# The opening loads of a one-core decoder layer, spread anew over two DMA queues

## The chip, the core and the metric

The kernel runs on one core of a Trainium2 chip. The metric is device time in microseconds for one execution. A core has five engines with instruction streams of their own: TensorE (PE in the profile; its weight loads are PEld), VectorE (DVE), ScalarE (ACT), GpSimd (POOL) and SyncE (SP). Transfers between the chip's main memory and the core's on-chip memory are issued as instructions in an engine's stream (SPq and ACTq in the profile are such issues on SyncE's and ScalarE's streams) and are then moved by 16 DMA engines, which serve both queues.

## The reference

One decoder layer over 256 tokens of width 2048, in float32: a norm, one wide projection, two parallel branches (a short convolution and a gated recurrence), a gated merge and an output projection, then a per-layer embedding and a final norm.

```python
    h = rmsnorm(x, norm_mix_g[i])
    u = h @ w_in[i]
...
    m = jax.nn.sigmoid(ga) * (ya @ w_a_out[i]) + jax.nn.sigmoid(gb) * (yb @ w_b_out[i])
    x = x + m @ w_o[i]
    gate = jax.nn.sigmoid(rmsnorm(x, ple_norm_g[i]) @ w_ple_gate[i])
    x = x + gate * (p[i] @ w_ple_proj[i])
return rmsnorm(x, final_norm_g)
```

The change concerns only how the inputs of `p[i] @ w_ple_proj[i]` reach the core. That product depends on nothing else, so the kernel does it first. `p` is 256 tokens by 256 features and `w_ple_proj` is 256 by 2048.

## The kernel before

**How a product is made.** Float32 accuracy comes from splitting each operand into a high part in the reduced format fp32r and the remainder. `cut` (lines 199 and 200) does this for weights: ScalarE copies the loaded tile `raw` to `whi`, then VectorE subtracts to get `wlo`. Each product is then three matmuls of 128 x 128 by 128 x 512: high by high, high weights by low operand, and low weights by high operand (lines 1157 to 1159). The contraction dimension goes in k tiles of 128.

**The list of weight pieces.** The weights are worked off as a fixed list of items, in an order written down in the code. Items 0 to 3 are the four groups of 512 columns of `w_pp` (`w_ple_proj`). Each is 128 partitions by 1024 numbers: the first 512 of a row belong to k tile 0 and the last 512 to k tile 1. The text calls the two halves of item 0 W0a and W0b, those of item 1 W1a and W1b, and so on to W3b; one half is 256 KB. `p` is laid out transposed with features on partitions. Its two k tiles, 128 KB each, are called p0 and p1; they go to the tile `praw`, and their split parts to `pop`.

**The first twelve matmuls** (line 1312) are those of item 0. For k tile 0 there are two matmuls (for two blocks of 128 tokens) with the high part of W0a and the high part of `pop`, two with the high part of W0a and the low part of `pop`, and two with the low part of W0a. The same six follow for k tile 1 with W0b and p1. Before these, TensorE runs eight matmuls on a zeroed tile `warm` (line 1046), which compute nothing that is used.

**Order on the engines.** Each engine works its own stream in order. ScalarE's stream starts with its DMA issues, then a load of its function table with a first activation (line 303), then the split of W0a, the high part of p1 (line 325), the split of W0b, W1a, W1b, W2a, W2b and, in one instruction, item 3. VectorE does the high part of p0 (line 323), its low part (line 326), and then the low parts in the same order as ScalarE. The parameters `prm_t` (norm gains, convolution weights and the like) are first read when the layer's input is split (line 328).

**A limit on transfers in flight.** The transfers that SyncE and ScalarE issue take turns over eight completion semaphores, DMAHW0 to DMAHW7. A transfer that uses a semaphore again waits, in its issuing engine's stream, until the transfer eight places before it has landed. The count runs over both queues together, roughly in the order of the program text.

Of the kernel before, what the change touches and what calls it, by code (L numbers as in the profile page):

```python
# [15 lines left out]
P = 128  # L16
T = 256
# [6 lines left out]
CW = 512  # L24
# [24 lines left out]
def hybrid_kernel(ctx, tc, xT, x, pT, prm, gfin, masks, w_in, w_a, w_b, w_o, w_pg, w_pp, out):  # L49
    nc = tc.nc  # L50
# [27 lines left out]
    def nm(s):  # L78
        uid[0] += 1
        return f"{s}_{uid[0]}"  # L80
# [26 lines left out]
    items = []  # L107
# [21 lines left out]
    def raw_of(pos):  # L129
        it = items[pos]  # L130
        if it["raw"] not in loaded:
            if it["kind"] == "S" and it["op"] == "hT":
                t = tuple(
                    pools["st"].tile([P, n, CW], F32, tag=tag, bufs=bufs, name=nm(tag))
                    for tag, n, bufs in (("sA", 2, 2), ("sB", 1, 3))
                )
            else:
                n = it["c"] if it["j"] == 0 else 4 + 4 * (it["j"] - 1) + it["c"] // 2
                spare = it["op"] == "x1T" and n in (5, 10, 14)
                pool, bufs = (pools["late"], 1) if spare else (wp, 3)  # L140
                t = pool.tile([P, 2, 2 * CW], F32, tag="raw", bufs=bufs, name=nm("raw"))
            loaded[it["raw"]] = t
        return loaded[it["raw"]]
# [117 lines left out]
    prm_t = const.tile([P, PRM_N], F32, name="prm_t")  # L261
    praw = pools["tmp1"].tile([P, 1024], F32, tag="X", bufs=4, name="praw")[:, : 2 * T]
# [10 lines left out]
    def load_half(pos, i, eng):  # L273
        w, g, c = items[pos]["w"]
        s = slice(i * CW, (i + 1) * CW)
        eng.dma_start(out=raw_of(pos)[:, pos % 2, s], in_=w[g, :, c, s])

    load_half(0, 0, nc.scalar)
    for k in range(2):
        nc.sync.dma_start(out=praw[:, k * T : (k + 1) * T], in_=pT[:, k, :])  # L280
    load_half(0, 1, nc.scalar)
    for i in range(2):
        load_half(1, i, nc.sync)
    nc.sync.dma_start(out=prm_t, in_=prm)
    for c in (2, 3):
        for i in range(2):
            load_half(c, i, nc.sync)
# [938 lines left out]
    for pos, it in enumerate(items[:last_group]):  # L1226
        mark, state["pos"] = len(nc.cur_bb.bb.instructions), pos
        kind, j, c, last = (it[n] for n in ("kind", "j", "c", "last"))
        _, _, w, g, opname = groups[it["gi"]]
# [71 lines left out]
        else:  # L1301
# [4 lines left out]
            for i in range(2):  # L1306
                k = 2 * c + i
# [50 lines left out]
    for t, halves in ((0, (0, 1)), (1, (0,)), (1, (1,))):  # L1358
        bk, n = bank("g"), CW // 2
        for c in range(nlast):  # L1360
# [4 lines left out]
            for i in range(2):  # L1365
                k = 2 * c + i
# [87 lines left out]
```

## Time and profile before

| | |
|---|---|
| median of 3 runs | 813.72 us (812.8 to 813.87) |
| profiled execution, its time | 812.97 us |
| profiled execution, its span | 811.2 us |
| TensorE busy | 801.2 us, 99% |
| VectorE, ScalarE, GpSimd busy | 605.9, 462.9, 55.0 us |
| first matmul whose result is used | 5.05 us after the span's start |

The span runs from the first to the last instruction in the trace; the time of an execution also has what lies around it, here 1.77 us. Rows of the timeline give the start, the duration, the engine, the line, the operation and the tiles, with a count where equal instructions were merged, and in square brackets how long the engine was idle before it and what ended that. A matmul's duration includes the pipeline, so the pace of TensorE is read from the distance of starts.

### The profile page before, as it was taken

The numbers are of one execution on the slowest core, as the hardware profiler recorded it, in microseconds if no ns is written. First come the engines' busy times: TensorE is split into PE (matmuls) and PEld (weight loads), VectorE is DVE, ScalarE is ACT, GpSimd is POOL, SyncE is SP. The second block draws the span as 40 slices with busy tenths as digits, with TensorE's granted clock in tenths as the row PEclk, the third lists the DMA queues.
The fourth block names the chain that finished last, engine by engine and source line by source line (L and its number), as shares of the span: only waits on it lengthen the run. The fifth ranks groups of instructions, "written<-read, shape, count | busy, mean of one in ns | idle before, by whom it ended". The sixth has DMA issues, their size and how long they took to land.

```text
span 811.2 us, 10709 instructions
## 1 busy us (share of the span) xinstructions
PE 801.2 (99%) x4053; PEld 663.7 (82%) x4053; DVE 605.9 (75%) x785; ACT 462.9 (57%) x624; POOL 55.0 (7%) x59
## 2 busy tenths in 40 slices
PE   9999999999999999999999999999999999999995
PEld 6888888888888888888888888888888888888885
DVE  6846588767776498767679987987988666789953
ACT  7676476465555466466456556556554446665733
POOL 1000000001000000000021210110000000000160
PEclk9999999999999999999999999999999999999999
DMA  9988555648767555647799996995844778896702
GB/s 337 392 312 292 194 204 170 230 141 267 256 236 257 182 187 200 207 160 261 271 313 309 305 327 206 304 329 194 249 158 174 284 271 277 309 349 245 297 27 103
DMA packets 54099, 198.52 MB, mean 245 GB/s; under 512 B 6944, under 2 KB 16928, under 8 KB 40352
## 3 DMA queue, kind: packets, MB, share of 16 engines
q1 hardware_dynamic: 44640, 174.78, 60.5%
q0 software_dynamic: 6384, 16.25, 8.4%
q10 hardware_dynamic: 3024, 6.82, 2.4%
q8 instruction: 31, 0.51, 0.2%
q14 instruction: 20, 0.16, 0.1%
HBM read 184.19 MB, written 13.63 MB: 244 GB/s over the span
## 4 chain that ended last, share of the span: by engine, by line
PE 98%; issue 1%; DMA 0%; ACT 0%; DVE 0%; POOLq 0%; POOL 0%
PE g L1157 27%; PE g L1158 27%; PE g L1159 27%; PE s L1157 5%; PE s L1158 4%; PE s L1159 4%; PE s L539 1%; DMA raw<-in_w_pp 0%; PE g L1312 0%; PE s L640 0%; PE s L659 0%; PE s L658 0%; PE s L657 0%; PE s L631 0%; ACT xs L1006 0%
## 5 line engine op out<-in xcount | busy, mean ns | idle before, releaser
L200 DVE TENSOR_TENSOR wlo<-raw,whi 128x1024 fp32r<-128x1024 f32 (+1 forms) x255 | 304.0, 1209 | 141.1 <-ACT whi L199 139.1
L199 ACT ACTIVATE whi<-raw 128x1024 fp32r<-128x1024 f32 (+1 forms) x255 | 262.1, 1045 | 186.8 <-PE g L1159 158.1
L1157 PE MATMUL g<-whi,xh 128*128 128x512 f32 (+1 forms) x656 | 253.1, 386 | 0.0
L1159 PE MATMUL g<-whi,xl 128*128 128x512 f32 (+1 forms) x656 | 252.7, 385 | 0.0
L1158 PE MATMUL g<-wlo,xh 128*128 128x512 f32 (+1 forms) x656 | 252.7, 385 | 0.0
L1159 PEld LDWEIGHTS g<-whi,xl 128*128 128x128 f32 x656 | 123.2, 188 | 24.9
L1157 PEld LDWEIGHTS g<-whi,xh 128*128 128x128 f32 x656 | 123.2, 188 | 24.6
L1158 PEld LDWEIGHTS g<-wlo,xh 128*128 128x128 f32 x656 | 123.2, 188 | 24.2
L1158 PE MATMUL s<-wlo,xh 128*128 128x512 f32 x120 | 46.7, 389 | 0.0
L1157 PE MATMUL s<-whi,xh 128*128 128x512 f32 x120 | 46.5, 389 | 0.0
L1159 PE MATMUL s<-whi,xl 128*128 128x512 f32 x120 | 46.5, 389 | 0.0
L1158 PE MATMUL g<-wlo,mh 128*128 128x512 f32 x112 | 43.6, 389 | 0.0
L1159 PE MATMUL g<-whi,ml 128*128 128x512 f32 x112 | 43.5, 390 | 0.0
L1157 PE MATMUL g<-whi,mh 128*128 128x512 f32 x112 | 43.1, 389 | 0.0
L199 ACT ACTIVATE thi<-sA 128x1024 fp32r<-128x1024 f32 x15 | 15.9, 1062 | 32.8 <-DVE sA L756 20.3
L1159 PEld LDWEIGHTS s<-whi,xl 128*128 128x128 f32 x120 | 22.5, 188 | 4.7
L1157 PEld LDWEIGHTS s<-whi,xh 128*128 128x128 f32 x120 | 22.5, 188 | 4.7
L1158 PEld LDWEIGHTS s<-wlo,xh 128*128 128x128 f32 x120 | 22.5, 188 | 4.7
L1158 PE MATMUL g<-wlo,ybTh 128*128 128x512 f32 x64 | 24.9, 389 | 0.0
L1159 PE MATMUL g<-whi,ybTl 128*128 128x512 f32 x64 | 24.9, 389 | 0.0
L1157 PE MATMUL g<-whi,yaTh 128*128 128x512 f32 x64 | 24.9, 389 | 0.0
L1158 PE MATMUL g<-wlo,yaTh 128*128 128x512 f32 x64 | 24.9, 389 | 0.0
(272 smaller groups left out, 1075.8 us busy)
## 6 DMA issues: line engine op xcount, KB each, us to landing
raw<-in_w_in SPq DMA_DIRECT2D x66, 1024.0 KB, 4.8
raw<-in_w_o SPq DMA_DIRECT2D x16, 1024.0 KB, 6.3
sT<-in_w_in POOLq DMA_DIRECT2D x30, 512.0 KB, 9.5
raw<-in_w_in SPq DMA_DIRECT2D x28, 512.0 KB, 5.7
raw<-in_w_a SPq DMA_DIRECT2D x8, 1024.0 KB, 7.8
raw<-in_w_b SPq DMA_DIRECT2D x8, 1024.0 KB, 8.7
raw<-in_w_pg SPq DMA_DIRECT2D x16, 512.0 KB, 6.6
raw<-in_w_pg SPq DMA_DIRECT2D x8, 1024.0 KB, 6.7
```

The lines of the kernel that those rows point to most:

```text
L199: a = nc.scalar.activation(out=hi, in_=src, func=AF.Copy)
L200: v = nc.vector.tensor_tensor(out=lo, in0=src, in1=hi.bitcast(F32), op=ALU.subtract)
L539: nc.tensor.matmul(out, X[:, 0, h, s], X[:, 1, h, t], start=True, stop=True, tile_position=(0, i * n))
L1157: nc.tensor.matmul(psum, oh, hi, start=first, stop=False)
L1158: nc.tensor.matmul(psum, oh, lo, start=False, stop=False)
L1159: nc.tensor.matmul(psum, ol, hi, start=False, stop=last)
```

## The change

Four things are changed in the opening loads. W0a, until now one transfer on ScalarE's queue, becomes two: partitions 0 to 95 on ScalarE's queue and partitions 96 to 127 on SyncE's. p1 moves from SyncE's queue to ScalarE's, ahead of W0b. The parameters move from SyncE's queue to the end of ScalarE's opening issues. All the other transfers keep their queue and order.

```diff
-    load_half(0, 0, nc.scalar)
-    for k in range(2):
-        nc.sync.dma_start(out=praw[:, k * T : (k + 1) * T], in_=pT[:, k, :])
+    def load_p(k, eng):
+        eng.dma_start(out=praw[:, k * T : (k + 1) * T], in_=pT[:, k, :])
+
+    def load_rows(i, eng):
+        r, (w, g, c) = (slice(0, 96), slice(96, P))[i], items[0]["w"]
+        eng.dma_start(out=raw_of(0)[r, 0, :CW], in_=w[g, r, c, :CW])
+
+    load_rows(0, nc.scalar)
+    load_p(0, nc.sync)
+    load_p(1, nc.scalar)
+    load_rows(1, nc.sync)
     load_half(0, 1, nc.scalar)
+    nc.scalar.dma_start(out=prm_t, in_=prm)
     for i in range(2):
         load_half(1, i, nc.sync)
-    nc.sync.dma_start(out=prm_t, in_=prm)
```

ScalarE's stream at the start of the program reads as follows before the change; `raw_85` holds items 0 and 1, `raw_93` items 2 and 3, and the wait in brackets names the semaphore.

```order
L276 DMA raw_85<-in_w_pp 128x512 x2
L303 ACT_TABLE_LOAD
L303 ACTIVATE table_113<-mhalf 128x8 [waits Pool_49]
L199 ACTIVATE whi_136<-raw_85 128x512 [waits DMAHW0_49]
L325 ACTIVATE pop<-praw 128x256 [waits DMAHW2_49]
L199 ACTIVATE whi_136<-raw_85 128x512 [waits DMAHW3_49]
L199 ACTIVATE whi_144<-raw_85 128x512 [waits DMAHW4_49]
```

The same place of ScalarE's stream after the change (line numbers behind the edit are 8 higher):

```order
L283 DMA raw_85<-in_w_pp 96x512
L279 DMA praw<-in_pT 128x256
L276 DMA raw_85<-in_w_pp 128x512
L290 DMA prm_t<-in_prm 128x72
L311 ACT_TABLE_LOAD
L311 ACTIVATE table_114<-mhalf 128x8 [waits Pool_49]
L199 ACTIVATE whi_137<-raw_85 128x512 [waits DMAHW2_49,DMAHW0_49]
L333 ACTIVATE pop<-praw 128x256 [waits DMAHW3_49]
L199 ACTIVATE whi_137<-raw_85 128x512 [waits DMAHW5_49]
L199 ACTIVATE whi_145<-raw_85 128x512 [waits DMAHW4_49]
```

Four issues instead of two stand ahead of the table load, and the split of W0a waits for two transfers instead of one.

SyncE's stream at the start of the program, before the change (`raw_98` is the first tile of `w_in`):

```order
L280 DMA praw<-in_pT 128x256 x2
L276 DMA raw_85<-in_w_pp 128x512 x2
L284 DMA prm_t<-in_prm 128x72
L276 DMA raw_93<-in_w_pp 128x512
L276 DMA raw_93<-in_w_pp 128x512 [waits DMAHW0_49]
L276 DMA raw_93<-in_w_pp 128x512 [waits DMAHW1_49]
L276 DMA raw_93<-in_w_pp 128x512 [waits DMAHW2_49]
L276 DMA raw_98<-in_w_in 128x512 [waits DMAHW3_49]
```

The same place of SyncE's stream after the change:

```order
L279 DMA praw<-in_pT 128x256
L283 DMA raw_85<-in_w_pp 32x512
L276 DMA raw_85<-in_w_pp 128x512 x2
L276 DMA raw_94<-in_w_pp 128x512 [waits DMAHW0_49]
L276 DMA raw_94<-in_w_pp 128x512 [waits DMAHW1_49]
L276 DMA raw_94<-in_w_pp 128x512 [waits DMAHW2_49]
L276 DMA raw_94<-in_w_pp 128x512 [waits DMAHW3_49]
L276 DMA raw_99<-in_w_in 128x512 [waits DMAHW4_49]
```

W1a and W1b now have 32 rows of W0a ahead of them instead of p1. There is one transfer more among the opening ones, so W2a is now the ninth of the count and waits for the first transfer to land, which it did not before; every later one waits for a transfer that is one place further back. The streams of TensorE, VectorE and GpSimd, and all of SyncE's and ScalarE's behind this place, are the same but for the numbering.

## The prediction

> **What bounds the kernel now.** I read the page first, its span, its busy times and the chain that ended last, since a change in the opening loads can only matter through what the chain shows at its start.
>
> ```profile
> span 811.2 us, 10709 instructions
> PE 801.2 (99%) x4053; PEld 663.7 (82%) x4053; DVE 605.9 (75%) x785; ACT 462.9 (57%) x624; POOL 55.0 (7%) x59
> PE 98%; issue 1%; DMA 0%; ACT 0%; DVE 0%; POOLq 0%; POOL 0%
> ```
>
> TensorE is the bound. Next come the chain in order of time, at its start, and the waits of TensorE over the whole span.
>
> ```profile
> 0.74 3.61 DMA raw<-in_w_pp
> 4.37 0.64 ACT whi L199
> 5.05 3.04 PE g L1312 x12
> 8.09 0.23 PE g L1157
> ```
>
> ```profile
> PE s L1046 <- DVE warm L1042: 1.2, 1, 1.2
> PE g L1312 <- ACT whi L199: 0.3, 1, 0.3
> ```
>
> So W0a's landing and its split set the first useful matmul at 5.05 us. From there on TensorE waits for nothing that the profile shows. Whatever moves the start, or opens a gap before the lead of the other engines has grown, moves the end by as much; anything else is hidden. The diff changes no other work, so the question is one of tenths of a microsecond. The timeline of that stretch, ScalarE and TensorE, shows how much there is to win or lose.
>
> ```profile
> 0.74 0.89 ACTq L276 DMA_DIRECT2D raw<-in_w_pp  x2
> 1.66 1.28 ACT L303 ACT_TABLE_LOAD   x1 [1.66 <-PEq L1443]
> 2.96 0.21 ACT L303 ACTIVATE table<-mhalf 128x8 f32<-128x8 f32 x1
> 4.37 0.63 ACT L199 ACTIVATE whi<-raw 128x512 fp32r<-128x512 f32 x1 [1.21 <-DMA raw<-in_w_pp]
> 4.96 0.42 ACT L325 ACTIVATE pop<-praw 128x256 fp32r<-128x256 f32 x1
> 5.36 0.63 ACT L199 ACTIVATE whi<-raw 128x512 fp32r<-128x512 f32 x1
> 6.42 2.08 ACT L199 ACTIVATE whi<-raw 128x512 fp32r<-128x512 f32 x3 [0.42 <-DMA raw<-in_w_pp]
> ```
>
> ```profile
> 1.19 3.59 PE L1046 MATMUL s<-warm 128*128 128x512 bf16 x8 [1.19 <-DVE warm L1042]
> 5.05 1.20 PE L1312 MATMUL g<-whi,pop 128*128 128x512 f32 x4 [0.27 <-ACT whi L199]
> 6.55 1.09 PE L1312 MATMUL g<-whi,pop 128*128 128x512 f32 x4
> 7.93 0.39 PE L1157 MATMUL g<-whi,pop 128*128 128x512 f32 x1
> ```
>
> The zero matmuls hold TensorE until 1.19 + 3.59 = 4.78, so an earlier W0a can win 5.05 - 4.78 = 0.27 us and no more. On the other side, W0b's split ends at 5.36 + 0.63 = 5.99, and TensorE needs it at 6.55: about 0.5 us of cover, counting the 0.05 us from a split's end to the matmul (4.37 + 0.63 = 5.00 to 5.05).
>
> **The change part by part.** The landing times come from the DMA issues, asked for in narrow windows (the last number is us from issue to landing; in the first window both were issued at 0.74, the ACTq row of the second is W0b, the praw row p1, the SPq row W1a).
>
> ```profile
> raw<-in_w_pp ACTq DMA_DIRECT2D x1, 256.0 KB, 3.6
> praw<-in_pT SPq DMA_DIRECT2D x1, 128.0 KB, 3.4
> ...
> raw<-in_w_pp ACTq DMA_DIRECT2D x1, 256.0 KB, 4.2
> raw<-in_w_pp SPq DMA_DIRECT2D x1, 256.0 KB, 4.7
> praw<-in_pT SPq DMA_DIRECT2D x1, 128.0 KB, 3.8
> ```
>
> W0a lands at 4.34, p0 at 4.14. W0b, issued second on ScalarE's queue, some 0.45 us after the first, lands at about 5.36, just when ScalarE is free for it. How the two queues share the engines is read from the DMA queues' packets in two stretches, 1.9 to 3.3 and 3.3 to 4.9 us (q10 is ScalarE's queue, q1 SyncE's; packets, MB, share).
>
> ```profile
> q10 hardware_dynamic: 122, 0.23, 45.3%
> q1 hardware_dynamic: 149, 0.14, 31.8%
> ...
> q10 hardware_dynamic: 165, 0.29, 54.7%
> q1 hardware_dynamic: 156, 0.16, 30.6%
> ```
>
> While W0a (rows of 2 KB) runs against p0 (rows of 1 KB), the queues move about as many packets each, but nearly twice the bytes on ScalarE's. So they take turns by packets rather than bytes.
>
> *W0a in two parts.* Its last 32 rows now stand behind p0's 128 rows: packet 160 of SyncE's queue. At 149 packets in 1.4 us, 106 per us, that is 1.5 us after the start; W0a's 128 packets now end at 122 / 1.4 = 87 per us, 1.47 us after the start. With each transfer's 16 further packets (two transfers make 122 + 165 = 287, 144 each) the counts are 192 and 144, so 1.8 and 1.65 us. The last rows thus land 0 to 0.15 later; I take +0.1, so the split at 4.47 and the first matmul at 5.15. The ends: -0.3, if bytes and not packets were shared (192 KB on each queue then, where p1 now shares W0a's time), and +0.45, if the 64 KB of the 32 rows go at SyncE's 0.14 / 1.4 = 0.1 MB per us (0.65 us behind p0, which lands 0.2 us before W0a).
>
> *Two more issues on ScalarE.* At 0.89 / 2 = 0.45 us each they push the table load from 1.66 to 2.55 and the first activation's end to 4.06. The idle 1.21 us before the split covers it; without that cover it costs up to 0.9 us. It also caps the gain: no split before 4.06.
>
> *p1 on ScalarE's queue.* Its 128 KB go behind 96 rows instead of behind p0 and beside W0a: landing 4.6 to 5.0 against 4.97. ScalarE needs it when W0a's split ends, 5.1, so nothing either way.
>
> *W0b behind p1.* Here lies the cost. ScalarE's queue must now move 96 + 128 + 128 = 352 rows until W0b is there, not 256. At 287 packets in 3.0 us, 96 per us, 96 more are +1.0 us. By bytes it is 576 KB against 512 at 0.52 / 3.0 = 0.17 MB per us: +0.4 us. The packet rows are nearer to the first, and W1a with its 2 KB rows is then the opponent on SyncE's queue, where p1 with 1 KB rows was; that could make it +1.4. I take +0.85: landing at 6.2, split until 6.84, matmul at 6.89 instead of 6.55, **+0.34 us**. The 0.1 us from W0a lies inside this, since the k tile 1 matmuls wait for the later of the two. The ends: 0 (+0.4 is under the cover of 0.5) and +0.9.
>
> *Behind it.* W1a has 64 KB instead of 128 ahead of it on SyncE's queue and lands no later; its split runs right after W0b's, 6.84 to 7.47, and TensorE wants it at 7.93 + 0.34 = 8.27. *The parameters* leave SyncE's queue: their issue is worth 0.43 us there, and the first reader stands far behind.
>
> ```profile
> 2.60 0.43 SPq L284 DMA_DIRECT2D prm_t<-in_prm  x1
> 3.07 0.43 SPq L276 DMA_DIRECT2D raw<-in_w_pp  x1
> ...
> raw<-in_w_pp SPq DMA_DIRECT2D x1, 256.0 KB, 4.8
> ...
> 4.37 0.80 SPq L276 DMA_DIRECT2D raw<-in_w_pp  x2
> ...
> 10.57 1.06 ACT L199 ACTIVATE whi<-raw 128x1024 fp32r<-128x1024 f32 x1 [0.79 <-DMA raw<-in_w_pp]
> 12.54 0.91 ACT L328 ACTIVATE xh<-t,prm_t 128x256 fp32r<-128x256 f32 x2 [0.42 <-DMA t<-in_xT]
> ...
> 10.65 0.39 PE L1157 MATMUL s<-whi,pop 128*128 128x512 f32 x1
> 13.37 0.39 PE L1157 MATMUL s<-whi,pop 128*128 128x512 f32 x1
> ```
>
> *One transfer more in the count of eight.* W2a, issued at 3.07 now, must wait for the first 96 rows, until 4.0 to 4.4. Even with the latency of 4.8 us that its issue now has it then lands by 9.2 and is split by 9.9; TensorE uses it at 10.65. What follows is issued one place, some 0.45 us, later: item 3's split would start at 11.0 instead of 10.57 and end at 12.1, against a use at 13.37. So this is hidden; the queue holds megabytes of work anyhow.
>
> **The sum.** W0a 0.1, which lies inside W0b's 0.34, and 0 for all the rest: +0.3 us. Against the profiled execution, 811.2 us of span and 1.77 around it, that is 813.3; its 812.97 lay 0.75 below the median of the runs, 813.72, and from that median I forecast 814.0. A measurement of this kernel can tell about 0.2% from no change, 1.6 us; this is 0.04%.
>
> The Trainium skill, "DMA: Bandwidth & Descriptors", section "Rules for kernel authors", says that two transfers to disjoint partitions are not worth it, because both are spread over the same 16 engines. The packet rows above fit that, as both queues were served in the same stretches; by this rule alone the split of W0a moves its landing by nothing, which is the second rival.
>
> **The rivals.** *The start is won (faster).* If the bytes are shared evenly, W0a lands up to 0.3 us earlier and W0b's delay stays under its cover. The 0.27 us idle before the first matmul speaks for it, the packet counts against it: -0.1 to -0.3, 813.5. It decides if W0b lands before 5.85 and W0a before 4.3. *Nothing moves.* W0a lands as now, W0b is late by less than 0.5: 813.7. For it speaks the byte rate of ScalarE's queue, which alone gives +0.4. *TensorE's clock comes up later.* The zero matmuls start 3.59 / 8 = 0.45 us apart, the later ones 0.23. If gaps of half a microsecond at 4.8 and 6.6 put the faster pace off by as long as the zero matmuls lasted, 3.6 us at half pace cost 1.8 us more: with the slip 816. Against it: the first four useful matmuls take 1.20 us together, the fast pace, in spite of the idle 0.27 ahead of them. The Trainium skill, "TensorE: Matmul & The Clock Gate", Part 1, names a window of about 3.4 us without work as what takes the clock back; by it gaps under 1 us would not, and no run here shows one yet.
>
> **How the numbers follow.** The slip of 0.1 to 1.0 us: 0.50. Nothing moves: 0.18. The start is won: 0.25. The clock or a much later landing: 0.07. Leaving out the last and some of the scatter of the runs (812.8 to 813.87), the range goes from the won start with low runs, 812.9, to the slip at its upper end with a late landing, 815.2. Beyond 0.2% lie only the clock case (0.05 of it) and, on the other side, 0.02 for something that the trace does not show, since the start has only 0.27 us to give.
>
> **What would show it.** Right: W0b's split starts between 5.8 and 6.8 on ScalarE, with an idle time before it ended by the transfer, and TensorE has a second wait of 0.1 to 0.9 us in the middle of the twelve matmuls. Table load at about 2.55, its activation over by 4.1. W2a issued behind the first landing, at 4.0 to 4.4, and no wait of TensorE after 9 us. Wrong: a first matmul before 4.95 with no gap behind it; starts 0.45 us apart in the first twelve; or a wait at items 2 or 3, if the count of eight costs more than I gave it.

## The result, and the profile after

The changed kernel takes 814.56 us (median of 21 runs, 813.62 to 817.84), the kernel before 813.02 us (median of 21, 812.74 to 815.47). The ratio is 1.0018, with an interval from 1.0013 to 1.0024: about 1.5 us more, five times the 0.3 us of the forecast. The time lies inside its range of 812.9 to 815.2.

The chain that ended last, at its start in the changed kernel, no longer runs through W0a (line numbers are 8 higher than before):

```profile
0.74 0.43 ACTq L283
...
1.20 0.45 ACTq L279
...
1.67 5.01 DMA raw<-in_w_pp
...
6.70 0.64 ACT whi L199
```

It runs through ScalarE's first issues to its third transfer, W0b, and the split of that. The waits of TensorE over the span show the same thing as a second, longer wait for a split on the same line, now that of W0b:

```profile
PE s L1054 <- DVE warm L1050: 1.2, 1, 1.2
PE g L1320 <- ACT whi L199: 1.0, 2, 0.7
```

ScalarE's timeline in the changed kernel, to be laid beside the one of before:

```profile
2.64 1.28 ACT L311 ACT_TABLE_LOAD   x1 [2.64 <-issue]
3.93 0.21 ACT L311 ACTIVATE table<-mhalf 128x8 f32<-128x8 f32 x1
4.38 0.63 ACT L199 ACTIVATE whi<-raw 128x512 fp32r<-128x512 f32 x1 [0.24 <-DMA raw<-in_w_pp]
4.92 0.40 ACT L333 ACTIVATE pop<-praw 128x256 fp32r<-128x256 f32 x1
6.70 2.79 ACT L199 ACTIVATE whi<-raw 128x512 fp32r<-128x512 f32 x5 [1.39 <-DMA raw<-in_w_pp]
```

W0a's split starts at 4.38 us, where it was 4.37. W0b's split starts at 6.70 instead of 5.36, behind an idle time of 1.39 us that the transfer ended. TensorE's timeline shows what that does, the last row being the first matmul on `w_in` (behind the four items of `w_pp`):

```profile
5.06 1.20 PE L1320 MATMUL g<-whi,pop 128*128 128x512 f32 x4 [0.35 <-ACT whi L199]
7.38 1.20 PE L1320 MATMUL g<-whi,pop 128*128 128x512 f32 x4 [0.67 <-ACT whi L199]
17.06 0.61 PE L1165 MATMUL g<-whi,xh 128*128 128x512 f32 x2
```

The same matmul on `w_in` in the kernel before:

```profile
16.09 0.62 PE L1157 MATMUL g<-whi,xh 128*128 128x512 f32 x2
```

The matmuls of k tile 1 start 0.83 us late (7.38 for 6.55), the first on `w_in` 0.97. This profiled execution took 813.81 us, 0.84 more than that of before: all of its loss is there by 17 us. It was among the quickest of the changed kernel's runs, so further traces of the same kernel were needed for the rest of the 1.5 us.

### The profile page after: what moved, and what is told of

It is laid out like the page before. It is cut to its first block, busy times and chain, and to the rows that moved or that the text cites. A ratio compares the mean times of both kernels' runs of the same rounds, so it can differ in the third digit from the quotient of the medians.

```text
span 812.0 us, 10711 instructions
## 1 busy us (share of the span) xinstructions
PE 801.3 (99%) x4053; PEld 663.7 (82%) x4053; DVE 605.4 (75%) x785; ACT 462.8 (57%) x624; POOL 55.0 (7%) x59
## 4 chain that ended last, share of the span: by engine, by line
PE 97%; issue 1%; DMA 1%; ACT 0%; DVE 0%; ACTq 0%; POOLq 0%; POOL 0%
PE g L1165 27%; PE g L1167 27%; PE g L1166 27%; PE s L1165 5%; PE s L1167 4%; PE s L1166 4%; DMA raw<-in_w_pp 1%; PE s L547 1%; PE s L648 0%; PE s L667 0%; PE s L666 0%; PE s L665 0%; PE g L1320 0%; PE s L639 0%; ACT xs L1014 0%
```

## The experiments

All ratios are to runs of the kernel before on the same chip, each with its 95% interval.

**More traces of both kernels.** The changed kernel without an edit, twice, and the kernel before once more.

> The changed kernel itself, once more, for a second trace of it. Its first trace has a span 0.8 us longer than before, but the median of its runs is 1.5 us longer. Theory 1 (W0b is late behind p1 on ScalarE's queue, and by how much differs from execution to execution): W0b's split starts after 6.2 us, TensorE has a wait in the middle of the twelve matmuls of 0.3 to 3 us, and the execution's time is that of before plus this wait plus 0.1 to 0.3. Rival (something else in the run differs, such as TensorE's pace): the wait accounts for less than half of what the execution is longer.

> The changed kernel once more, beside the two variants on the same chip, with a third trace. Theory: W0b lands between 6.5 and 7.4 us, and the profiled execution is longer than a fast execution of before (813.0) by W0b's landing less 5.9 us, plus 0.1 for the restart of TensorE and plus whatever waits of TensorE the trace shows elsewhere. Rival: the execution is longer by more than 0.5 us beyond that.

> The kernel before itself, for a second trace of it and as a measure of how far one trace differs from another. Theory: W0a and W0b land within 0.4 us of the first trace (4.34 and 5.36 us), TensorE has no wait in the middle of the twelve matmuls, no difference in time within 0.1%. Rival (the first trace was a lucky one): W0b lands after 6 us here too, with a wait of TensorE.

The changed kernel came out at 1.0023 (1.0014 to 1.0032) and 1.0019 (1.0010 to 1.0028), the kernel before at 1.0003 (0.9994 to 1.0012). The splits of W0a and W0b on ScalarE's timeline in the second trace of the changed kernel:

```profile
4.77 0.63 ACT L199 ACTIVATE whi<-raw 128x512 fp32r<-128x512 f32 x1 [0.63 <-DMA raw<-in_w_pp]
7.33 2.72 ACT L199 ACTIVATE whi<-raw 128x512 fp32r<-128x512 f32 x5 [1.62 <-DMA raw<-in_w_pp]
```

In its third trace:

```profile
4.87 0.63 ACT L199 ACTIVATE whi<-raw 128x512 fp32r<-128x512 f32 x1 [0.73 <-DMA raw<-in_w_pp]
7.41 2.20 ACT L199 ACTIVATE whi<-raw 128x512 fp32r<-128x512 f32 x4 [1.61 <-DMA raw<-in_w_pp]
```

And in the second trace of the kernel before:

```profile
4.39 0.63 ACT L199 ACTIVATE whi<-raw 128x512 fp32r<-128x512 f32 x1 [1.23 <-DMA raw<-in_w_pp]
5.42 0.64 ACT L199 ACTIVATE whi<-raw 128x512 fp32r<-128x512 f32 x1
```

So the two traces of before agree to 0.1 us, and those of the changed kernel do not: W0b's split starts at 6.70, 7.33 and 7.41 us, and the first matmul on `w_in` at 17.06, 17.66 and 17.73, that is 0.97, 1.57 and 1.64 us after the 16.09 of both traces of before. The middle one is the 1.5 us of the medians. The profiled executions took 813.81, 815.44 and 814.50 us against 812.97 and 813.00. The second is about 0.9 us above what its start explains. TensorE's timeline there has a further wait far behind, for a split of weights:

```profile
707.92 0.50 PE L1166 MATMUL g<-wlo,mh 128*128 128x512 f32 x1 [0.48 <-DVE wlo L200]
```

Such a late wait of 0.2 to 0.5 us, behind 400 us, stands in six of all fourteen traces, here and below. All six are of kernels with W0a in two parts, and three more traces of such kernels are without it; the five traces without the split have none. So the one transfer more may take part in it, which no run settles. With 0.1 us for the restart of TensorE, 0.3 us of that execution remain unexplained. The expectation of this trace was met for W0b and missed for the time: the wait in the middle of the twelve matmuls is 0.90 us, less than half of the 2.47 us by which the execution was longer, which was the rival's sign. The slow pace of TensorE, which the rival named, is not seen at the start: the first four matmuls took 1.20 us here too. W0a's split was 0.40 late, and the late wait took 0.48.

**One part of the change alone.** Against the kernel before: only p1 moved; only W0a split; only the parameters moved. The diffs from here on are abridged and written with the helpers of the changed kernel.

```diff
 load_half(0, 0, nc.scalar)
 load_p(0, nc.sync)
+load_p(1, nc.scalar)
-load_p(1, nc.sync)
 load_half(0, 1, nc.scalar)
```

> Only p1 is moved to ScalarE's queue, between W0a (whole, 128 partitions) and W0b; the parameters stay on SyncE's queue. Theory 1: this is the costly part; W0b lands at 6.2 us or later, +0.5 to +1.5 us on the kernel before. Rival (the 96/32 split costs, by its extra transfer or its later rows): no difference within 0.2 us.

```diff
-load_half(0, 0, nc.scalar)
+load_rows(0, nc.scalar)
 load_p(0, nc.sync)
+load_rows(1, nc.sync)
 load_p(1, nc.sync)
 load_half(0, 1, nc.scalar)
```

> Only the 96/32 split of W0a; p1 follows the 32 rows on SyncE's queue and the parameters stay there. Theory 1: W0b lands at 5.4 to 5.6 us as before or earlier, W0a within 0.1 us of before; no difference within 0.3 us (p1 64 KB later could cost up to 0.3). Rival (the split costs): +0.5 to +1.5 us.

```diff
 load_half(0, 1, nc.scalar)
+nc.scalar.dma_start(out=prm_t, in_=prm)
 for i in range(2):
     load_half(1, i, nc.sync)
-nc.sync.dma_start(out=prm_t, in_=prm)
```

> Only the parameters are moved to ScalarE's queue, as its third issue. Theory 1: the function table load is 0.45 us later and hidden; no difference within 0.2 us. Rival (ScalarE's longer row of issues costs): W0a's split starts later than 4.4 us behind the table, +0.3 us or more.

Measured: p1 alone 1.0016 (1.0007 to 1.0025); the split alone 1.0005 (0.9997 to 1.0014); the parameters alone 0.9999 (0.9991 to 1.0008). ScalarE's timeline with p1 alone moved:

```profile
5.84 0.42 ACT L332 ACTIVATE pop<-praw 128x256 fp32r<-128x256 f32 x1 [0.45 <-DMA praw<-in_pT]
7.21 2.72 ACT L199 ACTIVATE whi<-raw 128x512 fp32r<-128x512 f32 x5 [0.95 <-DMA raw<-in_w_pp]
```

And with the split alone:

```profile
4.64 0.63 ACT L199 ACTIVATE whi<-raw 128x512 fp32r<-128x512 f32 x1 [1.47 <-DMA raw<-in_w_pp]
5.56 0.42 ACT L333 ACTIVATE pop<-praw 128x256 fp32r<-128x256 f32 x1 [0.29 <-DMA praw<-in_pT]
```

p1 ahead of W0b on ScalarE's queue is what costs: by itself it puts W0b at 7.2 us and makes nearly all of the loss. The split by itself shows no gain and no clear loss; in its trace W0a's later part landed 0.2 us later than W0a before, and the first matmul on `w_in` came 0.34 us late, at 16.43. The parameters alone show no difference, within 0.1%.

**W0b ahead of p1.** Against the changed kernel:

```diff
 load_rows(0, nc.scalar)
 load_p(0, nc.sync)
+load_half(0, 1, nc.scalar)
 load_rows(1, nc.sync)
 load_p(1, nc.scalar)
-load_half(0, 1, nc.scalar)
```

> The changed kernel with W0b ahead of p1 on ScalarE's queue; all else as changed. Theory 1 (the place of W0b behind p1 in its own queue): W0b lands at 5.2 to 5.6 us, p1 now later, at 5.3 to 6.0, where ScalarE must wait for it since p1's split comes first; the time 0.3 to 1.0 us under the changed kernel's, 0.2 to 0.8 over before. Rival (the four issues on ScalarE's queue or the two parts of W0a): as slow as the changed kernel, 1.5 to 1.9 us over before.

It measured 1.0016 (1.0007 to 1.0025), some 1.3 us over before, where the theory gave at most 0.8. W0b lands at 5.0 us (issued at 1.19, 3.8 us), but now p1 is the late one. ScalarE's timeline:

```profile
6.60 0.42 ACT L333 ACTIVATE pop<-praw 128x256 fp32r<-128x256 f32 x1 [1.52 <-DMA praw<-in_pT]
6.92 2.18 ACT L199 ACTIVATE whi<-raw 128x512 fp32r<-128x512 f32 x4
```

p1 is half the size of W0b and lands at 6.58, now that it stands third. ScalarE works in order, so W0b, there since 5.0, waits behind it. Third place alone does not make p1 late: with W0a split alone, p1 also stands third, on SyncE's queue behind p0 and the 32 rows, and lands at 5.54.

**Why W0b in third place is so late.** Four kernels try bytes, rows and place. First, W0b and W1a exchange queues, so that fewer rows stand ahead of W0b:

```diff
-load_half(0, 1, nc.scalar)
+load_half(0, 1, nc.sync)
-load_half(1, 0, nc.sync)
+load_half(1, 0, nc.scalar)
```

> The changed kernel with W0b and W1a exchanged between the queues: SyncE moves p0, the 32 rows, W0b, W1b; ScalarE the 96 rows, p1, W1a and the parameters. Theory 1, by packets: W0b is 288 rows deep in its queue instead of 352, as it was 256 deep before, so it lands some 0.65 us earlier than in the changed kernel, at 5.8 to 6.5 us, and costs 0 to 0.7 us on the kernel before. Rival (what counts is the bytes that both queues hold in all, not the place): as the changed kernel, 6.6 to 7.3 us.

Second, W1a and W1b go behind W0b on ScalarE's queue:

```diff
-load_half(1, 0, nc.sync)
-load_half(1, 1, nc.sync)
+load_half(1, 0, nc.scalar)
+load_half(1, 1, nc.scalar)
-nc.scalar.dma_start(out=prm_t, in_=prm)
+nc.sync.dma_start(out=prm_t, in_=prm)
```

> The changed kernel with W1a and W1b moved behind W0b on ScalarE's queue, so that SyncE's queue has no 2 KB rows while W0b is moved (only the parameters, and W2a from its wait on); the split of W0a may start no earlier than 4.6 us behind ScalarE's five issues. Theory 1 in its part on the sharing (W0b is slowed by W1a's packets on the other queue): W0b lands at 5.0 to 5.6 us although p1 is ahead of it, and the wait in the middle of the twelve is under 0.2 us; W1a and W1b are then late instead, 6.5 to 7.5. Rival (the extra transfers ahead in its own queue alone hold W0b up): it lands after 6.2 us as in the changed kernel.

Third, the parameters stand opposite W0b in SyncE's third place instead of W1a:

```diff
 load_half(0, 1, nc.scalar)
-nc.scalar.dma_start(out=prm_t, in_=prm)
+nc.sync.dma_start(out=prm_t, in_=prm)
 for i in range(2):
     load_half(1, i, nc.sync)
```

> The changed kernel with one thing moved: the parameters (36 KB) are SyncE's third transfer, ahead of W1a and W1b, instead of ScalarE's fourth. W0b stays third on ScalarE's queue behind the 96 rows and p1. Theory 2, from the landings so far (a transfer lands when all bytes of its own and earlier turns in both queues are through: 640 KB 5.0 to 5.2 us, 768 KB 5.3 to 5.8, 1024 KB 6.2 to 7.3, 1280 KB 6.9 to 7.2): W0b's turn now holds 804 KB instead of 1024, so it lands at 5.4 to 6.0 us, and most of the loss is gone, within 0.5 us of before. Rival (what is ahead of it in its own queue holds W0b up): 6.6 to 7.3 us, +1.3 to +1.9 as the changed kernel.

Fourth, against the kernel before, only the 36 KB of the parameters between W0a and W0b:

```diff
 load_half(0, 0, nc.scalar)
 load_p(0, nc.sync)
 load_p(1, nc.sync)
+nc.scalar.dma_start(out=prm_t, in_=prm)
 load_half(0, 1, nc.scalar)
 for i in range(2):
     load_half(1, i, nc.sync)
-nc.sync.dma_start(out=prm_t, in_=prm)
```

> The kernel before with one thing moved: the parameters (128 rows of 288 bytes, 36 KB) stand on ScalarE's queue between W0a and W0b; p1 stays on SyncE's queue. W0b is third on its queue with 128 rows more ahead of it, as in the changed kernel, but with 36 KB instead of 128. If the transfers or rows ahead of W0b in its own queue hold it up: W0b lands at 6.3 to 7.3 us, +0.9 to +1.6 us over before, as moving p1 alone did. If it is the bytes: W0b lands at 5.4 to 5.8 us and the time is within 0.3 us of before.

In the table, the landing is the last of the 16 updates that a transfer makes to its completion semaphore in the trace; the column before it has the eighth of them.

| kernel | W0b's place, rows and KB ahead of it in its queue | eighth update, us | W0b lands, us | ratio (interval) |
|---|---|---|---|---|
| before, two traces | second; 128, 256 | 4.7, 4.8 | 5.3, 5.4 | 1 |
| split alone | second; 96, 192 | 4.8 | 5.2 | 1.0005 (0.9997 to 1.0014) |
| changed, three traces | third; 224, 320 | 5.8, 6.1, 6.1 | 6.7, 7.3, 7.4 | 1.0018 (1.0013 to 1.0024) |
| p1 alone | third; 256, 384 | 6.8 | 7.2 | 1.0016 (1.0007 to 1.0025) |
| exchanged queues | third; 160, 192 | 5.4 | 7.2 | 1.0021 (1.0012 to 1.0030) |
| parameters opposite | third; 224, 320 | 5.2 | 6.5 | 1.0012 (1.0003 to 1.0021) |
| small one ahead | third; 256, 292 | 6.2 | 8.3 | 1.0021 (1.0012 to 1.0031) |

W0b's split with the queues exchanged, and with the parameters opposite:

```profile
7.19 2.77 ACT L199 ACTIVATE whi<-raw 128x512 fp32r<-128x512 f32 x5 [1.73 <-DMA raw<-in_w_pp]
6.56 2.89 ACT L199 ACTIVATE whi<-raw 128x512 fp32r<-128x512 f32 x5 [1.13 <-DMA raw<-in_w_pp]
```

Neither the bytes nor the rows ahead order these landings: 192 KB ahead gave 5.2 in second place and 7.2 in third, and 160 rows no less than 256. W0b in third place landed 1.1 us or more behind W0b in second, of which about 0.5 is its later issue (1.67 us in the changed kernel, 1.18 before). But place is not the whole of it: p1, half as large, landed at 5.54 in the very place where W0b landed at 7.17, third on SyncE's queue behind p0 and the 32 rows, though what stood opposite differed too. The eighth update shows two parts. It lies between 5.2 and 6.8 us in third place, latest in the two kernels with 256 rows ahead. From there to the last update W0b took 0.4 us with p1 alone moved and 1.4 to 2.0 in the last three rows of the table: a tail that no count of rows or bytes gives.

The first of the four missed its count of packets (5.8 to 6.5) and landed in its rival's figure, the bytes of both queues (6.6 to 7.3). In the third, that sum of bytes (5.4 to 6.0) missed in turn, and the own queue (6.6 to 7.3) was off by little. Its trace is of the quickest of its 11 runs. Against the changed kernel's runs on the same chip its median is 0.5 us lower (814.35 for 814.84), so what stands opposite seems to take part too. In the fourth the bytes fell outright, and W0b was later than either number; that trace is of one of its slower runs (815.52, median 814.91). ScalarE's timeline there:

```profile
5.00 0.40 ACT L332 ACTIVATE pop<-praw 128x256 fp32r<-128x256 f32 x1
8.30 2.71 ACT L199 ACTIVATE whi<-raw 128x512 fp32r<-128x512 f32 x5 [2.90 <-DMA raw<-in_w_pp]
```

The second experiment told nothing of the sharing. W0b landed at 7.3 us there, after the 6.2 of the rival, but not for the reason to be tested. One more transfer on ScalarE's queue made its fifth issue the one that waits for the eighth before it, and so the table load behind it came at 4.93 us; also W2a moved up to 2.11 us on SyncE's queue and took W1a's part. ScalarE's timeline:

```profile
1.67 3.23 ACTq L276 DMA_DIRECT2D raw<-in_w_pp  x3
4.93 1.28 ACT L311 ACT_TABLE_LOAD   x1 [4.93 <-DMA praw<-in_pT]
6.22 0.21 ACT L311 ACTIVATE table<-mhalf 128x8 f32<-128x8 f32 x1
6.34 0.61 ACT L199 ACTIVATE whi<-raw 128x512 fp32r<-128x512 f32 x1
```

The first useful matmul came at 7.00 us, 1.95 later than before, behind an idle time of 2.27 us. Then TensorE's granted clock went down. In this row for 8.0 to 11.4 us the clock is the third number from the end (the pairs ahead of it are each engine's busy time and its instructions):

```profile
8.00:11.40 3.40, 3.40 (x9) 2.61 (x9) 2.95 (x6) 2.50 (x5) 0.00 (x0) 0.50 1.02 362
```

The matmuls there start 0.43 us apart instead of 0.23, and the first one on `w_in` came 3.57 us late, at 19.66. So the 1.0036 (1.0024 to 1.0049) holds two losses: the cover over the table load was used up, and in this execution the clock went down as well.

**One place further back.** ScalarE moves the 96 rows, p1, W1a, W0b:

```diff
 load_rows(0, nc.scalar)
 load_p(1, nc.scalar)
+load_half(1, 0, nc.scalar)
 load_half(0, 1, nc.scalar)
-nc.scalar.dma_start(out=prm_t, in_=prm)
-load_half(1, 0, nc.sync)
 load_half(1, 1, nc.sync)
+nc.sync.dma_start(out=prm_t, in_=prm)
```

> The changed kernel with W0b one turn further back: ScalarE moves the 96 rows, p1, W1a, W0b; SyncE p0, the 32 rows, W1b, the parameters. Theory 2: W0b's turn holds 1024 + 256 + 36 = 1316 KB, so it lands at 7.0 to 7.8 us; +0.3 to +0.9 us on the changed kernel, all of it a longer wait of TensorE in the middle of the twelve matmuls. Rival (the loss of the changed kernel does not come from W0b's landing): no difference from the changed kernel.

W0b landed at 7.5 us and the kernel measured 1.0023 (1.0013 to 1.0033). The landing is at most 0.2 us behind the changed kernel's two late traces, and its time cannot be told from the changed kernel's, so by itself it decides nothing between the theory and the rival.

**Does the landing set the time?** The expectation of the changed kernel's third trace gives a time from the landing: 813.0, plus the landing less 5.9, plus 0.1 for the restart. Put beside the profiled executions without a late wait it gives 813.9 for 813.81 and 814.6 for 814.50 (changed, first and third), 814.4 for 814.51 (p1 alone), 813.7 for 813.69 (parameters opposite) and 815.5 for 815.52 (small one ahead). With the late wait and another 0.1 added it gives 814.8 for 814.95 (exchanged queues) and 815.2 for 815.24 (one place further back). Only the changed kernel's second trace lies further off, by the 0.3 us named above.

## Why the prediction was right, and by how much it was off

The direction, the place and the mechanism held: a second wait of TensorE in the middle of the twelve matmuls, because W0b stands behind p1. What was off is the size of the term "W0b behind p1": +0.85 us on its landing was taken, with +1.4 as the end, and the three traces show +1.3, +1.9 and +2.0. Its cover of 0.5 us was right: 1.3 late gave 0.83 at the matmuls of k tile 1. The +0.85 lay between +1.0 by rows and +0.4 by bytes, both at a mean pace of the queue. The rows were the nearer of the two, and the tail of one transfer, shown below, is in neither.

That the time fell inside the range is in part luck. The forecast of 814.0 stood on the median of three runs, 813.72; the kernel before measured 813.02 in 21. The same 1.5 us on top of 813.72 would have been 815.3, just outside the range. The case that was given most, a slip of 0.1 to 1.0 us at 0.50, did not come either. What came, a much later landing, shared 0.07 with the clock. Of the signs, W0b's split started between 5.8 and 6.8 us in the first trace alone, and the second trace has a wait after 9 us.

- *W0a in two parts*, +0.1: the 96 rows and the 32 rows landed at 4.0 and 4.3 us in the first trace, and the split started 0.01 late; in the other two 0.4 and 0.5 late, at the end given for the worst case (+0.45). It hides inside the wait for W0b, as was said.
- *Two more issues on ScalarE*, 0: the table load came at 2.64 (2.55 forecast) and the activation behind it was over at 4.14, under its cover.
- *p1 and the parameters*, 0: p1 landed before ScalarE asked for it; the parameters alone measured 0.9999.
- *The count of eight*, 0: no trace of the changed kernel has a wait of TensorE between 9 and 700 us; whether the one at 707.92 us comes from the count stays open.
- *Not in the sum*: the first matmul behind a wait takes 0.34 us to the next one's start instead of 0.23, at 5.05 us in the kernel before as at 7.38 in the changed one, so a second wait costs 0.1 more than its length.
- *The rivals.* The won start did not come: W0a's split never started before 4.38 us in the changed kernel, and W0b was late. "Nothing moves" fell with the wait. TensorE's clock did not come up late in any of the three traces of the changed kernel: four matmuls took 1.19 or 1.20 us at both places. It did in other kernels, as the last section shows. The rule of the Trainium skill on transfers to disjoint partitions agrees with the split alone, 1.0005, where W0a's parts landed at 4.37 and 4.55 us and the whole before at 4.35.

The chance of 0.93 for a move within 0.2% left too little beyond it: the ratio is 1.0018, and its interval reaches 1.0024.

## What to carry to other kernels

In the opening of this kernel, what the second group of matmuls needs stands second, p1 on one queue and W0b on the other. Putting either of the two behind the other on one queue cost about 1.3 us, and 36 KB put ahead of W0b cost 1.8. So before a transfer is moved, ask which one it pushes back, and how much cover that one has; an estimate at the mean pace of a queue was too small here. A single trace of a start that hangs on landings can mislead: three traces of one kernel differed by 0.7 us at the same matmul, while two of the other agreed.

## What the runs showed of the hardware that was not expected

**A transfer waits for its last straggler.** In the kernel with the parameters opposite, ScalarE's queue (q10) had moved nearly all before 5 us, but W0b landed at 6.54. The DMA queues' packets from 5.0 to 6.5 us (packets, MB, share of 16 engines):

```profile
q1 hardware_dynamic: 275, 0.49, 91.5%
q10 hardware_dynamic: 16, 0.03, 5.0%
```

5.0% of 16 engines is 0.8 of one engine on average. Of the 16 updates of W0b's semaphore, 14 had come by 5.47 us and the last two came at 6.24 and 6.54, while SyncE's queue kept the engines busy with its later transfers. The same view with the small transfer ahead, 6.0 to 8.2 us, W0b landing at 8.28:

```profile
q1 hardware_dynamic: 405, 0.74, 94.5%
q10 hardware_dynamic: 37, 0.06, 7.8%
```

There 12 updates had come by 6.83 us, and the last four came between 7.44 and 8.28. A mean pace of the queue does not foresee such a tail. Why it forms, and why it was short with p1 alone moved (0.4 us behind the eighth update), no run here shows.

**TensorE's fast pace can come late without a wait.** With only the parameters moved, W0a was split at 4.19 us and TensorE went on almost without a pause, yet its first four matmuls took the slow pace. Its timeline:

```profile
4.87 2.02 PE L1319 MATMUL g<-whi,pop 128*128 128x512 f32 x4
6.73 0.63 PE L1319 MATMUL g<-wlo,pop 128*128 128x512 f32 x2
7.20 1.08 PE L1319 MATMUL g<-whi,pop 128*128 128x512 f32 x4
```

Four in 2.02 us against 1.20; six matmuls later it was 0.65 us behind the kernel before (7.20 for 6.55), although it had started 0.18 earlier. The Trainium skill, "TensorE: Matmul & The Clock Gate", Part 1, says that the window that decides is free-running and not tied to the kernel's start. The traces fit: their record of the granted clock has its first full value at 5.0 and 5.1 us in those of before and at 6.7 in this one, and between 4.3 and 7.2 over all fourteen, though the zero matmuls start at 1.19 in each. Three more traces took the slow pace in the first four matmuls: W0b ahead of p1 (2.08 us), exchanged queues (1.85) and small one ahead (1.98). There the wait for k tile 1 hid most or all of it. So the 0.18 us won at the start were lost again in this trace, and 0.65 us beyond them.

**An idle time of 2.3 us was followed by half the clock.** The row of 8.0 to 11.4 us above, with W1a and W1b behind W0b, is the case of the prediction's third rival, at a longer gap than it had in mind. Idle times of up to 1.4 us in the other traces were not followed by it. The rule of the Trainium skill that the prediction cites, from the same Part 1, asks for a window of about 3.4 us without work. This trace shows the loss behind 2.27 us, and where the two differ the trace decides.
